# Half of the up projection by Strassen's scheme: 11 block products instead of 12, with the weight sums on VectorE

## The chip, the cores and the metric

One Trainium2 chip, one core. The metric is the device time of one execution, in microseconds (us).

## The reference, cut to what matters

One layer of a streaming encoder runs for 256 prompt frames and 8 x 16 sample frames, 384 tokens in all, in float32. The change lies in the last third, the feed-forward part:

```
h2 = rmsnorm(x, norm_ffn_g)                       # 384 x 2048
up = h2 @ w_up                                    # 2048 x 11264
g_half, u_half = up[..., :5632], up[..., 5632:]   # gate, up
gc = causal_dwconv(g_half with state, ffn_dw_w, ffn_dw_b)   # 3 taps
x  = x + (silu(gc) * u_half) @ w_down             # 5632 x 2048
```

Everything before it (norm, one combined projection, a convolution branch, attention, an output projection `w_out`) stays as it is, except for what the `w_out` stage prepares.

## The kernel before, in words

The 384 tokens are three tiles of 128. A float32 product is made from three matmuls: every operand is split into a part `hi` in the reduced matmul format and a remainder `lo`, and hi x hi, hi x lo and lo x hi are added up in PSUM (lines 235 to 237). Activations stand as the stationary operand (128 x 128, one load per matmul), weights stream past as the moving operand (512 columns).

Weights come as **items**: 256 rows by 512 columns, 512 KB, in the order of the list `plan`. `fetch` (L124) loads an item into one of three `raw` buffers, on SP's queue. `split` (L135) makes `hi` by a cast on ScalarE (L139) and `lo` by a subtraction on VectorE (L140); there are two `hi`/`lo` pairs. `ahead(2)` (L190) keeps one item split while TensorE uses another. An item is worth 2 K blocks x 3 token tiles x 3 = 18 matmuls.

The feed-forward part (from L957) goes over 11 groups of 512 gate and 512 up columns. `up_jobs` (L1031) makes the gate half of a group in 8 items, then the up half in 8 items; ScalarE takes each PSUM tile out with the norm's scale (L1039). The rows are then turned (`turned`, L261): three transposes of 32 x 32 blocks on VectorE (L249), four DMAs to DRAM (L254) and one back (L259), both issued by GpSimd. On the turned gate, `fill` (L983) copies rows on ScalarE (L987) and GpSimd (L990 to L994), and `taps` (L997) does the convolution on VectorE (L1006, L1008) and the Silu on ScalarE. `product` (L1019) multiplies gate and up and splits the result on VectorE (L1022, L1027) and ScalarE. `after(n, fn)` has a step emitted n ticks later; a tick is 9 matmuls. The down projection (`down_jobs`, L1043) runs after groups 4, 8 and 10, over four, four and three groups; VectorE adds its PSUM tiles to `y` (L1047).

In the `w_out` stage, `wo_job` (L922) turns each 512 columns of the residual, scales them, and splits them into `xg` (L939 to L942), the stationary operand of the up projection.

TensorE's order is that of the program. The other engines' order is set by a scheduler when the kernel is built: by priority (`SPLIT_AHEAD`, `EVAC_AHEAD`) and by its own idea of when things are ready. On the chip each engine then runs its list strictly in that order.

Of the kernel before, what the change touches and what calls it, by code (L numbers as in the profile page):

```python
# [33 lines left out]
SPLIT_AHEAD, EVAC_AHEAD = 150, 60  # L34

# [5 lines left out]
def hybrid_step(  # L41
# [92 lines left out]

    def split(raw, o, by_row=False):  # L135
        hi = wp.tile([P, 2, 512], F32R, tag="hi", bufs=2, name="hi")
        lo = wp.tile([P, 2, 512], F32R, tag="lo", bufs=2, name="lo")
# [6 lines left out]

    def planned(w, k0, cols, nk, *more):
        for k in range(k0, k0 + nk, 2):
            for cl in (cols,) + more:
                plan.append([w[0, k * P:(k + 2) * P, c:c + n].rearrange("(k p) n -> p k n", p=P) for c, n in cl])

    def up_cols(g):  # L150
        return [[(512 * g, 512)], [(DFF + 512 * g, 512)]]
# [21 lines left out]
    for what, g in FFN_PLAN:  # L173
        if what == "up":
            for cols in up_cols(g):
                planned(w_up, 0, cols, 16)
# [13 lines left out]
    def ahead(n):  # L190
        while plan and len(ready) < n:
            with tc.high_priority(offset=SPLIT_AHEAD):
                if x_left and (len(plan) - v_last) in range(3, 14, 2):
                    load_x(x_left.pop(0), 2)
                ready.append(split(*fetch(plan.pop(0))))
# [16 lines left out]
    def gemm(jobs, sides=()):  # L212
        for js in jobs:
# [4 lines left out]
            for j, k in [(j, k + i) for k in range(0, js[0]["nk"], 2) for j in js for i in range(2)]:  # L218
                nb, n, nk, ps = len(j["ps"]), j["n"], j["nk"], j["ps"]
                kk = k % 2  # L220
                if kk == 0:
                    ahead(2)
                    hi, lo = ready.pop(0)
# [682 lines left out]
    xg = [p_x2.tile([P, 2, 4, NT], F32R, name=f"xg{g}") for g in range(4)]  # L906
    p_w, close_w = pool("norm2", side="right")
    ss2 = p_w.tile([P, NTT, 4], F32, name="ss2")
    r2 = p_w.tile([P, NTT], F32, name="r2")
    y = []  # L910
# [10 lines left out]

    def wo_job(n):  # L922
        box = []

        def ev(t, ps):
# [4 lines left out]
            jk = p_w.tile([P, 512], F32, tag="jk", bufs=1, name="jk2")  # L930
            nc.scalar.activation(jk[:], ys, AF.Square, accum_out=ss2[:, t, n:n + 1])

        def done():
            d = box[0].moved()

            def parts(m):
                v = d[:, :, :, m, :]
                g = col[:, R_FFN + 4 * n + m:R_FFN + 4 * n + m + 1]
                hi, lo = natural(xg[n][:, 0, m, :]), natural(xg[n][:, 1, m, :])  # L939
                nc.scalar.activation(v, v, AF.Identity, scale=g)  # L940
                nc.scalar.copy(hi, v)
                tt(lo, v, f(hi), op=ALU.subtract)  # L942
            for m in range(4):
                after(3 + m // 2, lambda m=m: parts(m))
            if n == 3:
                second_norm()
        return job("B", 16, grouped(mix), ev, done=done)

    def second_norm():
# [3 lines left out]
        newton_rsqrt(r2[:], p_w.tile([P, NTT], F32, name="r2s")[:], m2[:])  # L953

# [4 lines left out]
    sft = p_f.tile([P, 44, 32], F32, name="sft")  # L959
# [6 lines left out]
    quadrants_in(sft[:].rearrange("p a c -> p (a c)"), quadrants_out(sw, 352))  # L966
# [139 lines left out]
```

## Time and profile before

| | |
|---|---|
| median of 3 runs | 1996.56 us (1995.78 to 1997.12) |
| profiled execution, its time | 1996.37 us |
| its span | 1994.7 us |
| TensorE busy | 1986.0 us of the span, 9386 matmuls |
| VectorE busy | 1063.9 us, 53% |
| ScalarE busy | 769.8 us, 39% |
| GpSimd busy | 211.1 us, 11% |
| moved by DMA | 339.31 MB, 170 GB/s on average |
| granted TensorE clock | 1.0 in every slice |

The feed-forward part begins at about 912 us and lasts to the end. A mean duration of an instruction is that of its record, from its start to its end; two that follow each other on VectorE can overlap a little in the record. The time of a run is 1.7 us above its span.

### The profile page before, as it was taken

The numbers are of one execution on the slowest core, as the hardware profiler recorded it, in microseconds if no ns is written. First come the engines' busy times: TensorE is split into PE (matmuls) and PEld (weight loads), VectorE is DVE, ScalarE is ACT, GpSimd is POOL, SyncE is SP. The second block draws the span as 40 slices with busy tenths as digits, with TensorE's granted clock in tenths as the row PEclk, the third lists the DMA queues.
The fourth block names the chain that finished last, engine by engine and source line by source line (L and its number), as shares of the span: only waits on it lengthen the run. The fifth ranks groups of instructions, "written<-read, shape, count | busy, mean of one in ns | idle before, by whom it ended". The sixth has DMA issues, their size and how long they took to land.

```text
span 1994.7 us, 24618 instructions
## 1 busy us (share of the span) xinstructions
PE 1986.0 (100%) x9386; PEld 1675.8 (84%) x9386; DVE 1063.9 (53%) x1492; ACT 769.8 (39%) x1134; POOL 211.1 (11%) x470
## 2 busy tenths in 40 slices
PE   9999999999999999999999999999999999999999
PEld 9999888888888888888888888888888888888887
DVE  4478889647456347445454555343554554334543
ACT  5433354554325323445343434222433442223422
POOL 1001121100000002011211112000211120002100
PEclk9999999999999999999999999999999999999999
DMA  6565776664444448566656565444555564346553
GB/s 183 155 170 159 230 240 209 204 179 136 126 132 122 132 149 277 179 192 173 216 160 193 164 193 168 150 132 131 175 175 177 181 185 134 128 131 194 162 186 121
DMA packets 190781, 339.31 MB, mean 170 GB/s; under 512 B 15342, under 2 KB 65513, under 8 KB 190655
## 3 DMA queue, kind: packets, MB, share of 16 engines
q1 hardware_dynamic: 173175, 273.19, 45.1%
q0 software_dynamic: 17168, 64.42, 10.3%
q8 instruction: 73, 1.20, 0.3%
q14 instruction: 45, 0.37, 0.1%
q10 hardware_dynamic: 320, 0.14, 0.0%
HBM read 298.64 MB, written 39.51 MB: 170 GB/s over the span
## 4 chain that ended last, share of the span: by engine, by line
PE 96%; DVE 3%; issue 1%; DMA 0%; SPq 0%; POOL 0%; ACT 0%; DVEq 0%; POOLq 0%
PE acc L236 28%; PE acc L235 28%; PE acc L237 28%; PE acc L232 2%; PE acc L230 2%; PE acc L231 2%; DVE ut L500 1%; DVE lo L140 1%; PE misc L235 1%; PE misc L236 1%; PE misc L237 1%; PE misc L299 0%; DMA kc<-in_cache_k_dram 0%; PE misc L711 0%; PE misc L744 0%
## 5 line engine op out<-in xcount | busy, mean ns | idle before, releaser
L140 DVE TENSOR_TENSOR lo<-raw,hi 128x1024 fp32r<-128x1024 f32 (+2 forms) x481 | 579.5, 1205 | 816.9 <-ACT hi L139 816.8
L139 ACT CAST hi<-raw 128x1024 fp32r<-128x1024 f32 (+2 forms) x481 | 498.8, 1037 | 1069.2 <-PE acc L237 897.3
L236 PE MATMUL acc<-lo,xg 128*128 128x512 f32 x1056 | 410.9, 389 | 0.1
L237 PE MATMUL acc<-hi,xg 128*128 128x512 f32 x1056 | 410.8, 389 | 0.0
L235 PE MATMUL acc<-hi,xg 128*128 128x512 f32 x1056 | 410.8, 389 | 0.0
L235 PE MATMUL acc<-hi,hT 128*128 128x512 f32 (+1 forms) x704 | 270.4, 384 | 0.1
L236 PE MATMUL acc<-lo,hT 128*128 128x512 f32 (+1 forms) x704 | 265.6, 377 | 1.1 <-DVE lo L140 0.9
L237 PE MATMUL acc<-hi,hT 128*128 128x512 f32 (+1 forms) x704 | 265.6, 377 | 0.0
L236 PEld LDWEIGHTS acc<-lo,xg 128*128 128x128 f32 x1056 | 198.3, 188 | 41.8 <-DVE lo L140 0.5
L235 PEld LDWEIGHTS acc<-hi,xg 128*128 128x128 f32 x1056 | 198.3, 188 | 41.1
L237 PEld LDWEIGHTS acc<-hi,xg 128*128 128x128 f32 x1056 | 198.3, 188 | 40.9
L236 PE MATMUL acc<-lo,act 128*128 128x512 f32 x484 | 188.3, 389 | 0.0
L235 PE MATMUL acc<-hi,act 128*128 128x512 f32 x484 | 188.3, 389 | 0.0
L237 PE MATMUL acc<-hi,act 128*128 128x512 f32 x484 | 188.3, 389 | 0.0
L254 POOL DMA_DIRECT2D turn<-block x124 | 67.9, 554 | 929.7 <-DVE block L249 903.6
L236 PEld LDWEIGHTS acc<-lo,hT 128*128 128x128 f32 x704 | 132.3, 188 | 24.0 <-DVE lo L140 2.8
L235 PEld LDWEIGHTS acc<-hi,hT 128*128 128x128 f32 x704 | 132.2, 188 | 24.0 <-issue 1.8
L500 DVE SCALAR_TENSOR_TENSOR ut<-ext,cw,ut 128x384 f32<-128x384 f32 x240 | 149.1, 621 | 5.5
L237 PEld LDWEIGHTS acc<-hi,hT 128*128 128x128 f32 x704 | 132.1, 188 | 22.9
L235 PEld LDWEIGHTS acc<-hi,act 128*128 128x128 f32 x484 | 90.9, 188 | 18.9
L237 PEld LDWEIGHTS acc<-hi,act 128*128 128x128 f32 x484 | 90.9, 188 | 18.8
L236 PEld LDWEIGHTS acc<-lo,act 128*128 128x128 f32 x484 | 90.9, 188 | 18.8
(296 smaller groups left out, 2126.5 us busy)
## 6 DMA issues: line engine op xcount, KB each, us to landing
raw<-in_w_up_dram SPq DMA_DIRECT2D x176, 512.0 KB
raw<-in_w_in_dram SPq DMA_DIRECT2D x96, 512.0 KB
raw<-in_w_down_dram SPq DMA_DIRECT2D x88, 512.0 KB
turn<-block POOLq DMA_DIRECT2D x120, 192.0 KB, 4.2
block<-turn POOLq DMA_DIRECT2D x30, 768.0 KB, 5.7
raw<-in_w_in_dram SPq DMA_DIRECT2D x64, 256.0 KB
raw<-in_w_out_dram SPq DMA_DIRECT2D x32, 512.0 KB
raw<-in_w_att_out_dram SPq DMA_DIRECT2D x16, 512.0 KB
```

The costliest lines, as they stand in the source:

```text
L139: nc.scalar.copy(hi[:, k, :o], raw[:, k, :o])
L140: tt(lo[:, k, :o], raw[:, k, :o], f(hi[:, k, :o]), op=ALU.subtract)
L230: mm(o, hi[:, kk, s], ah, start=st, stop=False)
L231: mm(o, hi[:, kk, s], al, start=False, stop=False)
L232: mm(o, lo[:, kk, s], ah, start=False, stop=sp)
L235: mm(o, ah[:, s], hi[:, kk, :n], start=st, stop=False)
L236: mm(o, ah[:, s], lo[:, kk, :n], start=False, stop=False)
L237: mm(o, al[:, s], hi[:, kk, :n], start=False, stop=sp)
L254: nc.gpsimd.dma_start(d[:, :, i, :].rearrange("j r n -> r j n"), src[32 * i:32 * i + 32, :].rearrange("r (j n) -> r j n", j=4))
L500: stt(o, v, wc, o, op0=ALU.mult, op1=ALU.add)
```

## The change

In 2 of the 4 blocks of 512 K rows (`MIXED`, blocks 0 and 1) the gate and up columns of a group are computed together. Token tiles 0 and 1, the two K pairs of the block and the column halves gate/up form a 2 x 2 by 2 x 2 block product, which takes 7 block products instead of 8; token tile 2 keeps its 4. So 12 become 11, and per mixed block and group 72 matmuls become 66.

- **Activations.** `combined` makes the five sums of token blocks once, in the `w_out` stage, and splits them and the five plain blocks into `xm`. Only blocks 2 and 3 keep `xg`.
- **Weights.** `planned_mixed` makes 7 items of a mixed block where there were 4. Four of the seven are sums, added on VectorE before the split (`both`, `top`, `grown` twice). A mixed block takes 5 loads instead of 4 (one is loaded twice). Items now carry 12, 12, 6 (first phase), 12, 6 (second), 12, 6 (third) matmuls; items of blocks 2 and 3 still 18.
- **Buffers.** There is a third `hi`/`lo` pair, and `ahead(3)` in the feed-forward part.
- **Order.** A group runs in three phases: up columns with the sums (10 items, 132 matmuls), products that both halves need (4 items, 36), gate columns (8 items, 108). A group is 22 items and 276 matmuls, where it was 16 and 288. The K blocks go 0, 2, 1, 3.
- **Evacuation.** Results are put together from PSUM by nine VectorE steps and seven ScalarE steps per group, where there were six on ScalarE.
- **Down.** The down projection now runs over two groups at a time (four times) and three at the end: 60 PSUM tiles to add instead of 36. So groups 1, 2, 4, 6, 8 and 10 begin right behind another group, the other four behind a down projection.

```diff
+        def both(q):
+            sums[q] = new_sum[0](q)
+            tt(sums[q], held["b22"][:], single("b12", 4 * q, c2)[:], op=ALU.add)
+            return sums[q]
+
+        def top(q):
+            b = single("b11", 4 * q, c1)
+            tt(b[:], b[:], held["b12"][:], op=ALU.add)
+            return b
+
+        def grown(q, name):
+            tt(sums[q], sums[q], held[name][:], op=ALU.add)
+            return sums[q]
+
+        for q in ORDER:
+            if q in MIXED:
+                add(lambda q=q: single("b22", 4 * q + 2, c2))
+                add(lambda q=q: both(q))
+                add(lambda q=q: top(q))
+            else:
+                planned(w, 4 * q, [(c2, 512)], 4)
+        for q in MIXED:
+            add(lambda q=q: single("b11", 4 * q, c1))
+            add(lambda q=q: grown(q, "b11"))
+        for q in ORDER:
+            if q in MIXED:
+                add(lambda q=q: single("b21", 4 * q + 2, c1))
+                add(lambda q=q: grown(q, "b21"))
+            else:
+                planned(w, 4 * q, [(c1, 512)], 4)
...
-    FFN_PLAN = [("up", g) for g in range(5)] + [("down", (0, 1, 2, 3))]
-    FFN_PLAN += [("up", g) for g in range(5, 9)] + [("down", (4, 5, 6, 7))]
-    FFN_PLAN += [("up", g) for g in range(9, 11)] + [("down", (8, 9, 10))]
+    FFN_PLAN = [("up", 0)]
+    for n in range(0, 8, 2):
+        FFN_PLAN += [("up", n + 1), ("up", n + 2), ("down", (n, n + 1))]
+    FFN_PLAN += [("up", 9), ("up", 10), ("down", (8, 9, 10))]
...
+        def add_up():
+            box.append(block()[:, :1280].rearrange("p (j m n) -> p j m n", j=5, m=2))
+            s = [blocks(box[0][:, j]) for j in range(5)]
+            tt(s[0], of(1, 1), of(1, 0), op=ALU.subtract)
+            tt(s[1], of(0, 0), s[0], op=ALU.add)
+            tt(s[2], of(0, 1), s[1], op=ALU.subtract)
+            tt(s[3], of(0, 0), of(1, 0), op=ALU.subtract)
+            tt(s[4], of(2, 1), of(2, 0), op=ALU.subtract)
...
+        def q3(ps):
+            stt(rows("u")[:, 0], ps, scale[0], e0, op0=ALU.mult, op1=ALU.subtract)
+
+        def q2(ps):
+            stt(rows("u")[:, 1], ps, scale[1], e1, op0=ALU.mult, op1=ALU.subtract)
...
+        def q6(ps):
+            with tc.high_priority(offset=EVAC_AHEAD):
+                tt(e0, ps, e1, op=ALU.subtract)
+            for r, sc in ((rows("u")[:, 0], scale[0]), (rows("u")[:, 1], scale[1]),
+                          (rows("g")[:, 1], nr2[:, 1:2])):
+                stt(r, e0, sc, r, op0=ALU.mult, op1=ALU.add)
+            ups[g] = Turned(block, rows("u")).moved().rearrange("p i t q c -> p (i t) q c")
...
+        for q in ORDER:
+            if q in MIXED:
+                seq += [pairs(q, ("q3", 2), ("tu", 4)), pairs(q, ("p7", 3), ("tu", 8)), pairs(q, ("p5", 0))]
+            else:
+                seq += plain(q, "q3", "q2", "tu")
...
+            if q in MIXED:
+                seq += [pairs(q, ("tg", 9), ("p2", 6)), pairs(q, ("q4", 7))]
+            else:
+                seq += plain(q, "p2", "q4", "tg")
```

Two places show how VectorE's list moves. The first is a gate's convolution, in the middle of the stretch in which the next group runs. In the rows of before, `lo<-raw,hi` is the subtraction of a split and `gc` a tap; four splits stand ahead of the first tap:

```order
L140 TENSOR_TENSOR lo<-raw,hi 128x1024 x4
L1006 TENSOR_SCALAR gc<-extf_7701,fw,col 128x384
L1006 TENSOR_SCALAR gc<-extf_7702,fw,col 128x384
L1008 SCALAR_TENSOR_TENSOR gc<-extf_7701,fw,gc 128x384
L1006 TENSOR_SCALAR gc<-extf_7703,fw,col 128x384
L1006 TENSOR_SCALAR gc<-extf_7704,fw,col 128x384
L1008 SCALAR_TENSOR_TENSOR gc<-extf_7702,fw,gc 128x384
L140 TENSOR_TENSOR lo<-raw,hi 128x1024
```

And of the change, where L149 is the same subtraction, L186 a sum `grown`, L1106 and L1108 the taps:

```order
L1106 TENSOR_SCALAR gc<-extf_7716,fw,col 128x384
L1106 TENSOR_SCALAR gc<-extf_7717,fw,col 128x384
L186 TENSOR_TENSOR sums<-sums,raw 128x1024
L149 TENSOR_TENSOR lo<-raw,hi 128x1024
L1106 TENSOR_SCALAR gc<-extf_7718,fw,col 128x384
L149 TENSOR_TENSOR lo_6749<-raw,hi_6748 128x1024
L186 TENSOR_TENSOR sums<-sums,raw 128x1024
L1106 TENSOR_SCALAR gc<-extf_7719,fw,col 128x384
L1108 SCALAR_TENSOR_TENSOR gc<-extf_7716,fw,gc 128x384
L1108 SCALAR_TENSOR_TENSOR gc<-extf_7717,fw,gc 128x384
L149 TENSOR_TENSOR lo<-sums,hi 128x1024
```

What moved: splits and sums now stand between the taps, and from the first tap to the split of the group's 21st item there are 44 instructions in a row (16 splits and sums, 12 taps, 8 product steps, 8 evacuation steps).

The second place is the start of the feed-forward part, where the last block of the residual, `xg_6751`, is split (L942 before, L1032 in the change). Before:

```order
L115 TENSOR_TENSOR r_6756<-r_6756,r2s 128x3
L140 TENSOR_TENSOR lo<-raw,hi 128x1024 x5
L942 TENSOR_TENSOR xg_6751<-block,xg_6751 128x4x3x32 x4
L140 TENSOR_TENSOR lo<-raw,hi 128x1024 x2
L249 STREAM_TRANSPOSE block<-block 128x11x4x32
```

The change:

```order
L1046 TENSOR_SCALAR nr_6761<-r_6760 128x3
L149 TENSOR_TENSOR lo<-raw,hi 128x1024 x2
L186 TENSOR_TENSOR sums<-sums,raw 128x1024
L149 TENSOR_TENSOR lo_6749<-raw,hi_6748 128x1024
L149 TENSOR_TENSOR lo<-raw,hi 128x1024
L186 TENSOR_TENSOR sums<-sums,raw 128x1024
L1032 TENSOR_TENSOR xg_6751<-block,xg_6751 128x4x3x32 x4
L149 TENSOR_TENSOR lo<-sums,hi 128x1024
```

What moved: the split of `xg_6751` now stands behind the splits of items 7 to 10 of the first group (counted from 0), while item 8 is the first that uses `xg_6751`.

## Rows read from the trace of the kernel before

**Rows 1.** The page: busy times of TensorE and VectorE, and the chain that ended last.
```profile
PE 1986.0 (100%) x9386; PEld 1675.8 (84%) x9386; DVE 1063.9 (53%) x1492; ACT 769.8 (39%) x1134; POOL 211.1 (11%) x470
...
PE 96%; DVE 3%; issue 1%; DMA 0%; SPq 0%; POOL 0%; ACT 0%; DVEq 0%; POOLq 0%
```

**Rows 2.** Windows: stretch, then busy us (count) by engine, clock, DMA share, GB/s.
```profile
1100.00:1200.00 100.00, 100.00 (x443) 82.84 (x442) 51.75 (x67) 41.01 (x54) 14.49 (x33) 1.00 0.59 178
...
1300.00:1400.00 100.00, 100.00 (x443) 82.83 (x442) 37.24 (x37) 26.38 (x25) 0.00 (x0) 1.00 0.42 131
```

**Rows 3.** All waits of TensorE: line, releaser, us in total, times, longest.
```profile
PE misc L318 <- POOL ident masks.py:199: 2.5, 1, 2.5
PE acc L236 <- DVE lo L140: 0.9, 3, 0.5
PE acc L232 <- DVE lo L140: 0.5, 1, 0.5
```

**Rows 4.** Groups by form, 1000 to 1994 us: busy us, mean ns, idle before.
```profile
L140 DVE TENSOR_TENSOR lo<-raw,hi 128x1024 fp32r<-128x1024 f32 x242 | 296.3, 1224 | 493.7 <-ACT hi L139 493.7
L139 ACT CAST hi<-raw 128x1024 fp32r<-128x1024 f32 x242 | 255.2, 1055 | 577.8 <-PE acc L237 497.9 <-PE misc L237 57.5 <-issue 22.0
...
L1008 DVE SCALAR_TENSOR_TENSOR gc<-extf,fw,gc 128x384 f32<-128x384 f32 x80 | 45.7, 612 | 0.0
...
L249 DVE STREAM_TRANSPOSE block<-block 128x512 f32<-128x512 f32 x60 | 41.9, 709 | 22.1 <-ACT block L1039 22.1
...
L1027 DVE TENSOR_TENSOR act<-ac,act 128x384 fp32r<-128x384 f32 x44 | 22.6, 553 | 1.2
L1047 DVE TENSOR_TENSOR y<-acc,y 128x512 f32<-128x512 f32 x33 | 22.6, 691 | 9.0 <-PE acc L237 9.0
...
L1006 DVE TENSOR_SCALAR gc<-extf,fw,col 128x384 f32<-128x384 f32 x40 | 19.1, 478 | 6.4 <-POOL extf L994 5.7
```

**Rows 5.** VectorE's timeline, 1144 to 1169 us: start, us, instruction, idle before.
```profile
1144.06 0.70 DVE L249 STREAM_TRANSPOSE block<-block 128x512 f32<-128x512 f32 x1
...
1159.24 1.22 DVE L140 TENSOR_TENSOR lo<-raw,hi 128x1024 fp32r<-128x1024 f32 x1 [2.85 <-ACT hi L139]
1160.82 1.04 DVE L1006 TENSOR_SCALAR gc<-extf,fw,col 128x384 f32<-128x384 f32 x2 [0.35 <-POOL extf L994]
...
1163.91 1.22 DVE L140 TENSOR_TENSOR lo<-raw,hi 128x1024 fp32r<-128x1024 f32 x1
1165.05 2.73 DVE L1008 SCALAR_TENSOR_TENSOR gc<-extf,fw,gc 128x384 f32<-128x384 f32 x5
1167.69 1.22 DVE L140 TENSOR_TENSOR lo<-raw,hi 128x1024 fp32r<-128x1024 f32 x1
```

**Rows 6.** The turn's DMAs to DRAM (after L254) and back (after L259): time to landing.
```profile
DMA to landing us min/median/max: 3.1/4.2/6.0
...
DMA to landing us min/median/max: 4.4/5.6/6.9
```

**Rows 7.** GpSimd's timeline at the same gate's fill, then all 44 instructions of L992.
```profile
1159.73 0.79 POOL L992 COPY extf<-extf 128x16 f32<-128x16 f32 x1 [6.83 <-ACT extf L987]
1160.46 0.19 POOL L993 COPY extf<-extf 128x12 f32<-128x12 f32 x1
...
L992 POOL COPY extf<-extf x44: 193/394/842, 971.6 to 1879.9; 128x16 f32<-128x16 f32 x44
```

**Rows 8.** VectorE at the start of the feed-forward part, then the first use of xg.
```profile
935.59 2.13 DVE L942 TENSOR_TENSOR xg<-block,xg 128x384 fp32r<-128x384 f32 x4
...
L235 PE MATMUL acc<-hi,xg x55: 389/389/390, 912.8 to 949.5; 128*128 128x512 f32 x55
```

**Rows 9.** SP's queue, 1100 to 1900 us; then the page: GB/s in 40 slices.
```profile
SPq L130 <- DVE lo L140: 680.2, 189, 4.2
...
GB/s 183 155 170 159 230 240 209 204 179 136 126 132 122 132 149 277 179 192 173 216 160 193 164 193 168 150 132 131 175 175 177 181 185 134 128 131 194 162 186 121
```

More of the change, by code (lines that the diff above doesn't have):

```diff
@@ L147, in planned, with planned_mixed, add, single @@
             for cl in (cols,) + more:
-                plan.append([w[0, k * P:(k + 2) * P, c:c + n].rearrange("(k p) n -> p k n", p=P) for c, n in cl])
-    def up_cols(g):
-        return [[(512 * g, 512)], [(DFF + 512 * g, 512)]]
+                plan.append([rows_of(w, k, c, n) for c, n in cl])
+    sums, new_sum = {}, []
+    ORDER = [q for n in range(4) for q in (MIXED[n:n + 1] + tuple(sorted(set(range(4)) - set(MIXED)))[n:n + 1])]
+    def planned_mixed(w, c1, c2):
+        held = {}
+        def add(fn):
+            plan.append(lambda: split(fn(), 512))
+        def single(name, k, c):
+            held[name] = fetch([rows_of(w, k, c, 512)])[0]
+            return held[name]
+        def both(q):
[25 more added lines that the diff above has]
+                planned(w, 4 * q, [(c1, 512)], 4)
     V_COLS = [[(O_V + 344 * i, 344)] for i in range(3)]
@@ L194, in ahead @@
                     load_x(x_left.pop(0), 2)
-                ready.append(split(*fetch(plan.pop(0))))
+                item = plan.pop(0)
+                ready.append(item() if callable(item) else split(*fetch(item)))
     def grouped(tiles):
@@ L997, in taps @@
             def taps():
-                gcs = gates[g] = [p_f.tile([P, NT], F32, tag="gc", bufs=6, name="gc") for _ in range(4)]
+                gcs = gates[g] = [p_f.tile([P, NT], F32, tag="gc", bufs=4, name="gc") for _ in range(4)]
                 for w in range(3):
@@ L1011, in done @@
             after(5, taps)
+            after(7, lambda: product(g))
         return done
[L1014 to L1029 removed]
@@ L1031, in up_jobs, with product @@
-    def up_jobs(g):
-        def half(finish):
-            box = []
-            def ev(t, ps):
-                if t == 0:
-                    rows = block()[:].rearrange("p (t n) -> p t n", t=NTT)
-                    box.append(Turned(block, rows))
-                nc.scalar.activation(box[0].rows[:, t, :], ps[:], AF.Identity, scale=r2[:, t:t + 1])
-            return job("B", 16, xa, ev, done=finish(g, box))
-        return [half(up_g_done), half(up_u_done)]
+    def product(g):
+        act = acts[g] = gp.tile([P, 2, 4, NT], F32R, tag=f"G{1 + g % 3}", name=f"act{g}")
+        for m in range(4):
+            a = gates[g][m][:]
+            ac = a.rearrange("p (a c) -> p a c", c=32)
+            tt(ac, ups[g][:, :, m, :], ac, op=ALU.mult)
+            av = a.rearrange("p (i t c) -> p i t c", i=4, t=NTT)
+            hi, lo = natural(act[:, 0, m, :]), natural(act[:, 1, m, :])
+            nc.scalar.copy(hi, av)
+            tt(lo, av, f(hi), op=ALU.subtract)
@@ new lines, in hybrid_step, with run @@
+    spent = [0]
+    def run(seq, forms, bank, finish, open_=()):
+        last = {b: (i, n) for i, prods in enumerate(seq) for n, (b, _, _) in enumerate(prods)}
+        for i, prods in enumerate(seq):
+            ahead(depth[0])
+            hi, lo = ready.pop(0)
+            for n, (b, (ah, al), kk) in enumerate(prods):
+                st = b not in forms
+                if st:
+                    forms[b] = bank()
+                o = forms[b][:]
+                mm(o, ah, hi[:, kk, :], start=st, stop=False)
+                mm(o, ah, lo[:, kk, :], start=False, stop=False)
+                mm(o, al, hi[:, kk, :], start=False, stop=last[b] == (i, n) and b not in open_)
+            for b in last:
+                if last[b][0] == i:
+                    finish[b](forms[b][:])
+            spent[0] += len(prods)
+            while spent[0] >= 3:
+                spent[0] -= 3
+                tick(())
```

142 lines of the change are left out of this document (108 added, 34 removed).

## The prediction

> **What bounds the kernel now.** I read the page first: TensorE is busy over the whole span, and the chain that ended last is TensorE for 96% [rows 1]. The windows then show how fast it goes in the feed-forward part: 443 matmuls in 100 us at full clock, whether VectorE is busy for 52 or for 37 of them [rows 2]. That is 225.7 ns per matmul. The list of its waits shows that it practically never stands: 1.4 us in total for splits of VectorE [rows 3]. So matmuls are the price, and a matmul less is 225.7 ns less as long as the weights are split in time. VectorE's groups show the slack: before its 242 splits it idled 493.7 us, waiting for casts, and the casts idled 577.8 us, almost all of it until TensorE gave a buffer free [rows 4]. SP's loads, too, wait for splits, not the other way round [rows 9].
>
> **The change part by part.**
>
> *Matmuls.* 6 fewer per mixed block, 2 blocks, 11 groups: 132. 132 x 225.7 ns = **29.8 us less**.
>
> *Splits and sums.* 3 more splits and 4 sums per mixed block: 66 more casts, 66 more subtractions, 88 sums. A split costs VectorE 1.224 us and ScalarE 1.055 us [rows 4]; the sum has the same 1024 elements, and I give it 1.224 us as well. That is 14 x 1.224 = 17.1 us more of VectorE per group. Beside it come nine evacuation steps per group that VectorE did not have: an addition from PSUM takes 0.69 us [rows 4], and the multiply-and-add forms I put at 0.75, since on 384 elements that form takes 612 ns where a product step takes 553; 6.5 us. ScalarE gets 6 casts and one evacuation more per group, some 7 us, and its casts idled for more than half of the time. Nothing of this is on TensorE's path by itself. What hides it is the time that an item gives: a buffer comes free when TensorE ends the item three before, then 1.055 us of cast and 1.224 us of subtraction follow. An item used to be 18 x 0.2257 = 4.06 us; now there are items of 12 (2.71 us) and 6 (1.35 us).
>
> *Where that cover gets thin.* In six groups (1, 2, 4, 6, 8, 10) the gate of the group before is turned, filled and convolved inside the next group's items, which the order shows. I add up VectorE's list there, from the first tap to the split of item 20: 16 splits and sums 19.6 us, 8 taps of 612 ns 4.9 us, 4 of 478 ns 1.9 us, 8 product steps 4.4 us [rows 4], one transpose 0.7, two additions 1.4, five multiply-and-adds 3.75: **36.7 us**. TensorE's cover in the same stretch: VectorE is done with split 8 at the earliest 2.4 us after item 5 ends (cast, split, a hop of 0.1), and item 20 is due after items 6 to 19, which are 162 matmuls, 36.6 us: 34.2 us of cover. By full durations 2.5 us are missing. But records overlap: five taps in a row end with the next instruction starting 2.64 us after the first, 528 ns each where the record says 612, and a split that began at 1163.91 is followed at 1165.05, 1.14 us later [rows 5]. That is 85 ns less for each of 44: 3.7 us, so 33.0 us, and **1.2 us of slack**. I take this value, since it is measured on the same forms back to back, and keep 2.5 us missing as the other end.
>
> The Trainium skill speaks against it: "VectorE: DVE Perf Modes", section "The DRAIN you can't avoid", says that the next instruction does not start until the pipe of the one before is empty. By that rule the full durations count and the stall is 2.5 us per group; the trace has the next start inside the record of the last.
>
> *The gate's taps come late, too.* Between the last transpose of a gate and its first tap lie the turn through DRAM and the fill. Before: the transpose ends at 1144.76, the first tap starts at 1160.82, 16.1 us [rows 5]. In the change the transposes end about 4.4 us after the group (two evacuations of 0.75, three transposes of 0.71, a split of 1.22 between them, less 85 ns each), so taps can begin 20.5 us after it; VectorE reaches them after items 0 to 5 (78 matmuls, 17.6 us) plus 2.4, at 20.0. That is 0.5 us of standing. Landing varies: 3.1 to 6.0 us out, 4.4 to 6.9 back, medians 4.2 and 5.6 [rows 6]; with 18 loads in a 62 us group instead of 16 in 65 I take half the way to the maxima, 1.55 us more. So 2.05 us late against 1.2 us of slack: 0.85 us of stall, six times, **5 us more** (bounds: 0, and 2.5 + 0.5 + 3.1 = 6.1 each, 37 us).
>
> *Start of the feed-forward part.* The last four steps of the residual's split now stand behind split 10 on VectorE, and split 10 needs the buffer of item 7; item 8 needs that residual. So after item 7 TensorE waits for a cast, a split and one step: 1.055 + 1.224 + 0.55 + hops, **3.0 us more**, once. Before, that split ran at 935.6 to 937.7 us, 23 us after the first up matmul at 912.8, when it was due after 12 K blocks (108 matmuls, 24.4 us) [rows 8]; now it is due after 96 (21.7 us). Bounds 0 to 4.
>
> *The w_out stage.* Two residual blocks get 11 steps on VectorE instead of 4. Nine of 256 elements and one of 1280 stand between two splits: by the 1.14 us of 1024 and the 470 ns of 384, some 4.4 to 5.3 us. The splits there come every 4.06 us with 1.8 us to spare. 0 to 0.6 us each, I take **0.6 us more** in all.
>
> *Costed at nothing.* The 24 more additions of the down projection (0.69 us each) fall into stretches where VectorE is busy for 37 of 100 us [rows 2]; if the cover were gone they would cost 17 us. The 22 more loads of 512 KB wait in SP's queue for buffers: three raw buffers are now held for the sums, so the loads come in bunches, three in 30 matmuls (6.8 us), 232 GB/s, and one slice of before has 277 GB/s with TensorE busy throughout [rows 9]. SP's small stores of gate rows stand where the raw buffer of the next load is still held, so they hold up nothing. The last down projection needs the last group's product after 8 items (32.5 us), and by the chain above it is ready at about 31.8: 0 to 3 us, taken as 0.
>
> Sum: -29.8 + 5 + 3.0 + 0.6 = -21.2. Against the profiled execution, 1996.37 us (0.2 below the median of the runs): **1975 us**.
>
> **The rivals.**
>
> *A. VectorE's instructions do not overlap in this list* (chance 0.17). This is the rule cited above. Waits between engines stand between most of them, and the overlap of rows 5 is one of instructions that waited for nothing. Then 2.5 + 0.5 = 3.0 us per group, with half the landings 4.5: 18 to 27 us. -29.8 + 3.6 + 22 = -4: 1992 us. For it: full records. Against it: the 1.14 us of a split among taps.
>
> *B. The gate comes late, and VectorE's list blocks on it* (chance 0.12): slower. The first tap stands in front of splits in a list that runs strictly in order, so each microsecond that a gate is late beyond the slack is a microsecond of TensorE, six times. It decides from (29.8 + 4.0 - 3.6) / 6 = 5 us of stall per group. Landings at their maxima give 3.1 us. GpSimd's fill gives the rest: a copy of 0.19 us took 0.79 us when a split ran on VectorE, and ended as the split ended; the 44 copies of that line lie between 193 and 842 ns [rows 5, 7]. Four copies stand ahead of the first tap, each up to 1.14 us later: 4.6 us. 0.5 + 3.1 + 4.6 - 1.2 = 7.0 per group, 42 us: -29.8 + 3.6 + 42 = +16, 2012 us. Against it: VectorE stands idle between splits 7 and 8, just when the fill runs.
>
> The Trainium skill, "SBUF — State Buffer", section "SBUF: two separate sides", has a rule for such copies: a GpSimd instruction and a VectorE instruction with two inputs in SBUF exclude each other for a whole instruction. The trace agrees, with 0.79 us beside a split.
>
> *C. The loads come late* (chance 0.06). Of 22 bunches of three loads each costs 1 us: -21.2 + 22, 1997 us. Against it: SP waits only for splits, 680 us in 800 [rows 9].
>
> *D. All is hidden* (chance 0.10): 1996.4 - 29.8 = 1966.6 us.
>
> **How the numbers follow.** The forecast has 0.55, with a range of its own of 1967 to 1985. A measurement of this kernel can tell 0.2% from no change, 4.0 us. Faster by more: forecast, D and about 0.10 of A, 0.75. Within: the rest of A and most of C, 0.12. Slower: B and a little of C, 0.13. The range, 1966 to 1994, holds the forecast, A and D, 0.82.
>
> **What would show it.** The page should count about 9254 matmuls (9386 before); a window inside a down projection still has 443 matmuls in 100 us. TensorE's waits should name the split's subtraction (L149) for some 5 us in groups 1, 2, 4, 6, 8, 10 at their items 12 to 20, and the residual's split (L1032) once for about 3 us. VectorE's busy time should be near 1063.9 + 154 x 1.22 + 24 x 0.69 + 99 x 0.72 = 1340 us, two thirds of the span. Waits on VectorE for GpSimd before the first tap should be about 0.5 to 2 us in those groups; 7 us there would be rival B. Subtractions that follow taps at 1.22 us and not 1.14 would be rival A. The prediction is wrong if TensorE waits over 15 us in all, or if a matmul takes longer than 226 ns among the short items.

## The result, and the profile after

The changed kernel takes 2007.18 us (median of 5 runs, 2003.84 to 2007.23), the kernel before 1996.56 us (5 runs beside it). The ratio is 1.0048, with a 95% interval from 1.0033 to 1.0062: slower by half a per cent, about 10 us. The forecast was 1975 us, and with it faster. The profiled execution took 2007.18 us, its span 2005.5 us against 1994.7 us before: 10.8 us more.

The page: busy times of the engines, and the chain that ended last, as in [rows 1].

```profile
PE 1973.6 (98%) x9254; PEld 1652.7 (82%) x9254; DVE 1317.8 (66%) x1784; ACT 841.5 (42%) x1216; POOL 227.6 (11%) x470
...
PE 80%; DVE 11%; DMA 5%; issue 2%; POOL 1%; ACT 1%; SPq 0%; DVEq 0%; POOLq 0%; ACTq 0%
```

The 132 matmuls are gone (9254 of 9386), but 20% of the chain is no longer TensorE; before it was 4%. What TensorE waited for (line, releaser, us in total, times, longest), against [rows 3]:

```profile
PE acc L289 <- DVE y L1233: 9.9, 8, 1.8
PE acc L1139 <- DVE lo L149: 5.3, 7, 2.2
PE acc L1138 <- ACT xg L1031: 3.0, 1, 3.0
PE misc L1139 <- DVE lo L149: 2.9, 5, 0.8
...
PE acc L1140 <- DVE xg L1032: 1.3, 1, 1.3
```

The largest wait is one that the forecast had put at nothing: the first matmuls of a job of the down projection (L289) wait for the additions of y (L1233), which let a PSUM bank go. The splits (L149, 8.2 us in the two rows shown) come second, the late residual (L1031, L1032) third. The windows of the changed kernel, as in [rows 2]: the first five stages of the feed-forward part, and two stretches inside them.

```profile
914.20:1111.80 197.60, 192.25 (x830) 156.44 (x829) 158.09 (x190) 100.45 (x129) 37.26 (x71) 0.98 0.63 197
1111.80:1183.10 71.30, 68.95 (x289) 55.72 (x288) 40.52 (x53) 22.67 (x29) 9.12 (x22) 0.95 0.50 167
1183.10:1309.40 126.30, 125.53 (x554) 103.55 (x553) 95.94 (x107) 58.97 (x69) 13.88 (x30) 1.00 0.57 175
1309.40:1378.00 68.60, 66.04 (x289) 53.79 (x288) 40.41 (x53) 22.68 (x29) 9.11 (x22) 1.00 0.52 169
1378.00:1507.20 129.20, 126.98 (x553) 103.24 (x552) 95.64 (x107) 58.91 (x69) 16.57 (x30) 1.00 0.55 171
...
939.70:946.50 6.80, 5.34 (x12) 3.79 (x13) 4.11 (x6) 3.47 (x8) 0.00 (x0) 0.50 0.52 161
...
1147.90:1154.70 6.80, 6.25 (x15) 4.46 (x14) 4.37 (x8) 0.65 (x2) 0.00 (x0) 0.50 0.24 77
```

A down projection of two groups has 288 matmuls and takes 65.3 us where nothing waits (e4, below), 226.7 ns for each; here the first takes 71.3 us and the other three 68.7. And the granted clock, 1.00 throughout the kernel before, is 0.50 in two stretches of 6.8 us and one of 3.4 us (from 1864.7): 1.2 GHz instead of 2.4. Each goes with a stand of TensorE: one of 3.2 us that ended at 939.8, one of 1.9 that ended at 1146.3, one of 2.3 that ended at 1864.3. In the stretches of 6.8 us the windows count 12 and 15 matmuls, where full clock gives 30; in the first of them TensorE also stood for another 1.7 us.

All runs can be read by one table, worked out from the profiled executions: the time from the first matmul of a stage to the first of the next, the four two-group downs added up, and groups 3 to 10 as well. The first line is e4 (below), which has the stages of the change with the matmuls of before, less 226.7 ns for each that the change removes: what the change would take if nothing waited more. Each line is one execution. The runs of one kernel lie 1 to 9 us apart, so differences of 2 or 3 us outside the downs can be chance.

| kernel | stage starts | groups 0 to 2 | four downs | groups 3 to 10 | last down |
|---|---|---|---|---|---|
| e4 less removed matmuls | 912.6 | 188.1 | 261.1 | 500.5 | 97.9 |
| the change | 914.2 | 197.6 | 277.4 | 513.4 | 98.4 |
| e1 | 912.2 | 197.7 | 261.1 | 508.3 | 98.4 |
| e12 | 913.2 | 200.2 | 261.1 | 510.3 | 98.3 |
| e2 | 912.9 | 196.2 | 277.4 | 510.4 | 98.4 |
| e3 | 912.4 | 207.6 | 266.2 | 515.2 | 97.9 |
| e5 | 912.5 | 196.3 | 261.1 | 509.8 | 98.3 |
| e6 | 912.9 | 197.6 | 261.1 | 507.9 | 97.9 |
| e7 | 912.3 | 195.6 | 261.1 | 510.5 | 98.4 |
| e8 | 913.2 | 195.4 | 261.1 | 508.9 | 98.4 |
| e9 | 913.9 | 195.8 | 261.1 | 505.6 | 97.9 |
| e10 | 912.1 | 195.5 | 261.1 | 506.8 | 98.4 |
| e11 | 912.0 | 194.8 | 261.1 | 504.2 | 97.9 |

So the change saves 29.9 us of matmuls and gives back 16.3 us in the downs, 12.9 in groups 3 to 10, 9.5 in groups 0 to 2 and 2.1 at the two ends: +10.9 us, where the spans say 10.8.

### The profile page after: what moved, and what is told of

The parts are those of the page before. It is cut to its first block, busy times and chain, and to the rows that moved or that the text cites. A ratio compares the mean times of both kernels' runs of the same rounds, so it can differ in the third digit from the quotient of the medians.

```text
span 2005.5 us, 24794 instructions
## 1 busy us (share of the span) xinstructions
PE 1973.6 (98%) x9254; PEld 1652.7 (82%) x9254; DVE 1317.8 (66%) x1784; ACT 841.5 (42%) x1216; POOL 227.6 (11%) x470
## 4 chain that ended last, share of the span: by engine, by line
PE 80%; DVE 11%; DMA 5%; issue 2%; POOL 1%; ACT 1%; SPq 0%; DVEq 0%; POOLq 0%; ACTq 0%
PE acc L289 15%; PE acc L291 15%; PE acc L290 15%; PE acc L1140 6%; PE acc L1139 6%; PE acc L1138 6%; DVE lo L149 4%; DMA raw<-in_w_up_dram 3%; PE misc L1139 3%; PE misc L1140 3%; PE misc L1138 2%; DVE ut L554 2%; PE acc L286 2%; PE acc L284 1%; PE acc L285 1%
## 5 line engine op out<-in xcount | busy, mean ns | idle before, releaser
L149 DVE TENSOR_TENSOR lo<-raw,hi 128x1024 fp32r<-128x1024 f32 (+2 forms) x481 | 577.2, 1204 | 505.7 <-ACT hi L148 503.3
L289 PE MATMUL acc<-hi,hT 128*128 128x512 f32 (+1 forms) x704 | 270.4, 384 | 0.1
L290 PE MATMUL acc<-lo,hT 128*128 128x512 f32 (+1 forms) x704 | 266.2, 378 | 1.3 <-DVE lo L149 1.2
L289 PE MATMUL acc<-hi,act 128*128 128x512 f32 x484 | 190.8, 394 | 10.0 <-DVE y L1233 9.9
L1139 PE MATMUL acc<-lo,xg 128*128 128x512 f32 x440 | 173.4, 394 | 3.8 <-DVE lo L149 3.7
L1138 PE MATMUL acc<-hi,xg 128*128 128x512 f32 x440 | 173.4, 394 | 3.1 <-ACT xg L1031 3.0
L1140 PE MATMUL acc<-hi,xg 128*128 128x512 f32 x440 | 172.8, 393 | 1.3 <-DVE xg L1032 1.3
L289 PEld LDWEIGHTS acc<-hi,hT 128*128 128x128 f32 x704 | 132.2, 188 | 24.0 <-issue 1.8
L148 ACT CAST hi<-sums 128x1024 fp32r<-128x1024 f32 x66 | 69.4, 1051 | 127.3 <-PE misc L1140 43.5
L1139 PE MATMUL acc<-lo,xm 128*128 128x512 f32 x308 | 120.3, 391 | 1.6 <-DVE lo L149 1.6
L1138 PE MATMUL acc<-hi,xm 128*128 128x512 f32 x308 | 119.9, 389 | 0.0
L1140 PE MATMUL acc<-hi,xm 128*128 128x512 f32 x308 | 119.9, 389 | 0.0
L289 PEld LDWEIGHTS acc<-hi,act 128*128 128x128 f32 x484 | 91.5, 189 | 33.9 <-ACT hi L148 8.6
```

The lines of the kernel that those rows point to most:

```text
L148: nc.scalar.copy(hi[:, k, :o], raw[:, k, :o])
L149: tt(lo[:, k, :o], raw[:, k, :o], f(hi[:, k, :o]), op=ALU.subtract)
L289: mm(o, ah[:, s], hi[:, kk, :n], start=st, stop=False)
L290: mm(o, ah[:, s], lo[:, kk, :n], start=False, stop=False)
L1138: mm(o, ah, hi[:, kk, :], start=st, stop=False)
L1139: mm(o, ah, lo[:, kk, :], start=False, stop=False)
```

## The experiments

Line numbers shift with the edits; the operation and the names say which line is meant.

### The down projection: e4, e1, e12

e4 is the kernel before with the change's `FFN_PLAN` (its diff stands above).

> The kernel before with nothing changed but the grouping of the down projections (pairs of groups instead of four, four and three). It has 24 more additions and pairs of jobs that end after 8 items instead of 16, but its taps lie in the second half of a group and its products early in the down, some 20 us ahead of the pair's end. Theory (it is the meeting of taps and products with the end of the pair that costs): 1996 to 1999 us, waits for additions under 2 us in all. Rival (smaller downs cost by themselves, by additions or bank release): 2006 to 2010 us, four pairs of gaps as in the changed kernel.

Measured: 1996.10 us, ratio 1.0001 (0.9992 to 1.0010). The list of waits has none of TensorE in the feed-forward part, and the down takes 65.3 us:

```profile
1108.80:1174.10 65.30, 65.30 (x290) 54.09 (x289) 32.25 (x38) 19.47 (x22) 2.74 (x5) 1.00 0.48 154
```

So neither the 24 additions nor the smaller downs cost anything that can be measured by themselves. One thing of the expectation was off: the products come at 1127 to 1133 us, and the pair's first additions at 1136.2, some 3.5 us later and not 20.

In the changed kernel they meet. VectorE there, in the first two-group down (start, us, instruction): 

```profile
1139.84 2.73 DVE L1108 SCALAR_TENSOR_TENSOR gc<-extf,fw,gc 128x384 f32<-128x384 f32 x5
1142.49 1.02 DVE L1120 TENSOR_TENSOR gc<-block,gc 128x384 f32<-128x384 f32 x2
1143.43 1.22 DVE L149 TENSOR_TENSOR lo<-raw,hi 128x1024 fp32r<-128x1024 f32 x1
1144.56 1.02 DVE L1124 TENSOR_TENSOR act<-gc,act 128x384 fp32r<-128x384 f32 x2
1145.50 0.68 DVE L1233 TENSOR_TENSOR y<-acc,y 128x512 f32<-128x512 f32 x1
1146.10 0.55 DVE L1120 TENSOR_TENSOR gc<-block,gc 128x384 f32<-128x384 f32 x1
1146.57 0.68 DVE L1233 TENSOR_TENSOR y<-acc,y 128x512 f32<-128x512 f32 x1
1147.17 1.21 DVE L149 TENSOR_TENSOR lo<-raw,hi 128x1024 fp32r<-128x1024 f32 x1
1148.30 0.68 DVE L1233 TENSOR_TENSOR y<-acc,y 128x512 f32<-128x512 f32 x1
```

And TensorE:

```profile
1144.19 0.39 PE L291 MATMUL misc<-hi,act 128*128 128x512 f32 x1
1146.33 0.47 PE L289 MATMUL acc<-hi,act 128*128 128x512 f32 x1 [1.75 <-DVE y L1233]
...
1149.04 0.80 PE L289 MATMUL acc<-hi,act 128*128 128x512 f32 x1 [0.55 <-DVE y L1233]
```

The first bank of the pair's first job was complete at 1139.1 (the end of its last matmul), but its addition stands behind taps, splits and product steps until 1145.50, and the second and third are pulled apart by another product step and a split. The pair holds all five banks of its pool and one of the other, so the third job's three banks are those of the first: it starts 1.91 us late, when the first addition is done, and waits 0.93 us more for the third. The same pair of gaps comes back in the other three downs, at 1343.9, 1541.8 and 1739.2.

e1 takes the need for that bank away:

```diff
-        return [(jobs[0], jobs[1])] + jobs[2:]
+        return [(jobs[0], jobs[1])] + jobs[2:] if last else jobs
...
-                j["ps"] = [(misc_tile if j is not js[0] and i == 2 else acc_tile)() for i in range(nb)]
+                j["ps"] = [(misc_tile if (j is not js[0] or j["spread"]) and i == 2 else acc_tile)()
```

> The changed kernel, but the four two-group down projections run their four column jobs one after the other (not the first two interleaved), and each job takes its third bank from the other PSUM pool, so that a job's first matmul never needs a bank that the job just before it still holds. Theory (bank release behind taps and products on VectorE): the four pairs of gaps of 1.91 and 0.93 us before L289 go, 11.4 us, and with them the half-clock stretch after 1146 (3.4 us): 2007 to 1992-1996 us, no wait of TensorE for the additions of y over 0.3 us. Rival 1 (VectorE has simply too much to do there, so the lateness moves on to the splits): the waits for the additions go, waits for splits in the same downs take their place, time within 3 us of 2007. Rival 2 (the clock falls whatever TensorE waits for): gaps go, three half-clock stretches stay, about 1996.

Measured: 1986.86 us (1984.01 to 1987.67), ratio 0.9957 (0.9940 to 0.9973): 20 us less than the change, more than expected. The gaps and the half-clock stretch in the first down are gone, 16.3 us in the table, and no other wait has come in their place there, so rival 1 falls. Of the three half-clock stretches one stays, at 938 us, so rival 2 falls as well. Groups 3 to 10 are 5 us shorter too, among other things without the half-clock stretch at 1864.7; why they vary by a few us between kernels that are alike there was not traced.

e12 leaves the banks and moves the taps:

```diff
-            after(5, taps)
-            after(7, lambda: product(g))
+            wait = 16 if g in (2, 4, 6, 8) else 0
+            after(5 + wait, taps)
+            after(7 + wait, lambda: product(g))
...
+                            if g in (2, 4, 6, 8):
+                                tc.add_manual_dep(d.ins, pair_end[0], mybir.DependencyInfo(
+                                    mybir.DependencyClass.NoSync, mybir.DependencyReason.DATA), reason="queue")
```

> The changed kernel with nothing but this: in the groups that a down projection follows (2, 4, 6, 8), taps and products stand behind the additions of the down's first pair of jobs on VectorE. Banks, pairing and the number of additions stay as in the changed kernel. Theory (the meeting of taps and products with the end of the pair is what costs): the four pairs of gaps of 1.91 and 0.93 us before L289 fall under 0.3 us, as in e4_plan_alone, and the half-clock stretch after 1146 goes: 1992 to 1997 us. Rival (the pair's five plus one banks are too few in the changed kernel, whenever the taps come): gaps stay, 2005 to 2008 us.

Measured: 1988.63 us, ratio 0.9956 (0.9940 to 0.9973), some 3 us below the range that was expected: the downs alone give back 16.3 us, where 14.8 had been added up from gaps and clock, and the rest was not traced. The downs take 65.3 us each, with the same six banks and the same additions. VectorE's list there, with the additions (L1238) now in front:

```profile
1140.81 2.05 DVE L1238 TENSOR_TENSOR y<-acc,y 128x512 f32<-128x512 f32 x3 [0.41 <-PE acc L291]
...
1144.89 1.37 DVE L1238 TENSOR_TENSOR y<-acc,y 128x512 f32<-128x512 f32 x2 [0.41 <-PE acc L291]
1146.25 0.69 DVE L1238 TENSOR_TENSOR y<-misc,y 128x512 f32<-128x512 f32 x1
1146.86 0.86 DVE L1107 TENSOR_SCALAR gc<-extf,fw,col 128x384 f32<-128x384 f32 x2
```

The additions start as their matmuls end. So it is the order in VectorE's list at the end of the pair that costs, and either cure, other banks or later taps, is enough.

### The start: e2, e5

ScalarE in the changed kernel, where the last block of the residual has been on its way back since 929.8:

```profile
936.01 1.05 ACT L148 CAST hi<-raw 128x1024 fp32r<-128x1024 f32 x1 [2.13 <-DMA raw<-in_w_up_dram]
937.30 1.04 ACT L148 CAST hi<-raw 128x1024 fp32r<-128x1024 f32 x1 [0.24 <-DMA raw<-in_w_up_dram]
938.25 1.12 ACT L1028 ACTIVATE block<-block,col 128x384 f32<-128x384 f32 x2
939.27 0.91 ACT L1031 CAST xg<-block 128x384 fp32r<-128x384 f32 x2
```

The residual's steps (L1028, L1031) stand behind two casts that themselves waited for loads. e2 orders the splits from the tenth item on, and the sums beside them, behind those steps on both engines:

```diff
+    def behind(d):
+        if last_part and len(skipped) >= 3:
+            tc.add_manual_dep(d.ins, last_part[d.ins.engine], mybir.DependencyInfo(
+                mybir.DependencyClass.NoSync, mybir.DependencyReason.DATA), reason="queue")
...
-            nc.scalar.copy(hi[:, k, :o], raw[:, k, :o])
-            tt(lo[:, k, :o], raw[:, k, :o], f(hi[:, k, :o]), op=ALU.subtract)
+            behind(nc.scalar.copy(hi[:, k, :o], raw[:, k, :o]))
+            behind(tt(lo[:, k, :o], raw[:, k, :o], f(hi[:, k, :o]), op=ALU.subtract))
```

> The changed kernel, with the splits of the items from the tenth on (and the sums beside them) ordered behind the last residual split on ScalarE and VectorE, at the start of the feed-forward part only. Theory (the residual's split stood behind casts and a sum that waited for late loads): the two gaps of 3.16 and 1.74 us at 940 us shrink to one of 1.5 to 2.5 us, since the turned residual lands at about 936; the half-clock stretch of 6.8 us there goes as well: 2007 to 1999-2002 us. Rival (the residual itself is late, its place in the list costs nothing): 2005-2007 us, gaps and half-clock stretch stay.

Measured: 2000.51 us, ratio 1.0027 (1.0016 to 1.0037). ScalarE reaches the residual at 936.09, and what TensorE waited for there is this:

```profile
PE acc L1151 <- ACT xg L1043: 2.2, 1, 2.2
PE acc L1151 <- ACT block L1192: 1.7, 1, 1.7
```

The gaps of 3.16 and 1.74 us became one of 2.35, and the half-clock stretch at 940 us, worth some 2.4 us, did not come. But two new gaps did: 1.16 us at 943.4, behind a split, and 1.88 us at 960, where an evacuation on ScalarE (L1192) now stands behind the casts that were held back. So groups 0 to 2 are shorter by 1.4 us only. The medians differ by 6.7 us; the rest of what the two profiled executions show lies ahead of group 0 (1.3) and in groups 3 to 10 (3.0), and is not shown to come from the edit.

e5 is e1 and e2 together.

> The edits of e1_down_single and e2_start_order together. If the two costs are separate they add: 20 us (e1) and 6.7 us (e2) below 2007: 1980 us, no half-clock stretch inside the feed-forward part or one at most, and about 12 us of TensorE's gaps left, most of them in groups 2, 4, 6, 8 and 10. Rival (the stalls of the start were only covered up by something that now comes to light): 1984 us or more.

Measured: 1983.33 us, ratio 0.9938 (0.9923 to 0.9953), no stretch of half clock before TensorE's last matmul. That is 3.5 us less than e1 where 6.7 were expected, near the rival's bound, and the intervals of e1 and e5 overlap: how much the second edit adds is open.

### The groups behind another group: e3, e6 to e11

VectorE stands waiting for loads in the changed kernel (its waits after 910 us), where before it had no such row:

```profile
DVE raw L182 <- DMA raw<-in_w_up_dram: 29.5, 16, 5.0
DVE sums L177 <- DMA raw<-in_w_up_dram: 14.1, 10, 3.6
```

and L186 adds 11.6 us. In groups 6, 8 and 10 most of TensorE's lost time comes behind such a stand. In group 10, VectorE and then TensorE:

```profile
1861.85 1.23 DVE L186 TENSOR_TENSOR sums<-sums,raw 128x1024 f32<-128x1024 f32 x1 [2.21 <-DMA raw<-in_w_up_dram]
1862.99 1.22 DVE L149 TENSOR_TENSOR lo<-raw,hi 128x1024 fp32r<-128x1024 f32 x1
1864.26 0.50 PE L1139 MATMUL acc<-lo,xg 128*128 128x512 f32 x1 [2.17 <-DVE lo L149]
```

The split of item 9 had its cast done at 1860.24, but stands behind a sum that waits for its load; TensorE stands for 2.3 us, and the half-clock stretch of 3.4 us follows. In groups 4, 6 and 8 TensorE waits at item 12 as well, 0.93 us each time, and there VectorE's list has run without a break since its first taps (groups 6 and 8) or the sum behind them (group 4). So two causes were open: late loads (theory L), or a list on VectorE that is too long (theory V). e3 adds a fourth buffer:

```diff
-        raw = wp.tile([P, 2, 512], F32, tag="raw", bufs=3, name="raw")
+        if fourth:
+            fourth.append(0)
+        if fourth and len(fourth) % 4 == 0:
+            raw = fourth[0]
+        else:
+            raw = wp.tile([P, 2, 512], F32, tag="raw", bufs=3, name="raw")
...
+    fourth.append(p_f.tile([P, 2, 512], F32, name="raw4")[:])
```

> The changed kernel with a fourth buffer for loaded weights in the feed-forward part, in room that three constants of earlier stages leave. Theory (a load of a mixed block is issued only when a sum has let a buffer go, and the sum of the next buffer then waits for it, so load latency lies in series): VectorE's waits for loaded weights (55 us on L177, L182 and L186) fall under 15 us, the stalls of groups 2, 4, 6, 8 and 10 fall from about 10 us to 3 or less: 2007 to 1998-2002 us; the gaps in the downs stay. Rival (VectorE's own time is short there, as by full durations): waits for loads fall, the stalls stay, 2005-2007 us.

Measured: 2007.68 us, ratio 1.0061 (1.0046 to 1.0076): nothing gained in all. The waits for loads did not fall; they rose to 91 us, and the order of the list moved too: the downs are 11.2 us shorter than in the change, groups 0 to 2 10.0 longer. VectorE in e3, group 10:

```profile
1845.72 1.22 DVE L155 TENSOR_TENSOR lo<-sums,hi 128x1024 fp32r<-128x1024 f32 x1
1853.84 1.23 DVE L192 TENSOR_TENSOR sums<-sums,raw 128x1024 f32<-128x1024 f32 x1 [6.90 <-DMA raw<-in_w_up_dram]
1854.98 2.35 DVE L155 TENSOR_TENSOR lo<-raw,hi 128x1024 fp32r<-128x1024 f32 x2
```

A sum that isn't due yet waits 6.9 us for its load, and two splits that are due stand behind it. So e3 tells nothing between L and V. e7 keeps splits and sums in the order of their items, e8 adds the fourth buffer to it:

```diff
+        e = d.ins.engine
+        if third and e in in_list:
+            tc.add_manual_dep(d.ins, in_list[e], mybir.DependencyInfo(
+                mybir.DependencyClass.NoSync, mybir.DependencyReason.DATA), reason="queue")
+        if third:
+            in_list[e] = d.ins.name
```

> e5 with the splits and weight sums of the feed-forward part kept in the order of the items on VectorE and ScalarE (no sum ahead of a split of an earlier item). Theory L1 (a sum that waits for a late load stands ahead of splits that are due first, as at 1853.8 in e3_raw4): VectorE's waits of sums for loads fall from 50 to under 35 us, 2 to 5 us less than e5. Theory V: within 2 us of e5.

> e7 with the fourth buffer for loaded weights of e3_raw4. Theory L2 (load latency lies in series behind the sums, and e3 lost what it won only by its order): VectorE's waits for loads under 20 us, 4 to 8 us less than e7. Theory V: waits for loads fall, the time is within 2 us of e7.

Measured: e7 1985.36 us, ratio 0.9949 (0.9934 to 0.9964); e8 1983.12 us, 0.9936 (0.9919 to 0.9952). Neither differs from e5, so the gains that L1 and L2 had forecast did not come. In e7 VectorE's waits for loads fell to 14 us, and in e8 the list of its waits has no row with a load at all. TensorE's waits at items 2 to 9 of groups 1 to 10 are gone in both. But now it waits at items further on, in e8 twice in each of groups 4, 6, 8 and 10. Group 6 of e8, which begins at 1429.2, VectorE and then TensorE:

```profile
1448.16 1.22 DVE L171 TENSOR_TENSOR lo<-raw,hi 128x1024 fp32r<-128x1024 f32 x1 [1.50 <-ACT hi L170]
1450.05 1.04 DVE L1136 TENSOR_SCALAR gc<-extf,fw,col 128x384 f32<-128x384 f32 x2 [0.66 <-POOL extf L1124]
...
1453.23 0.48 DVE L1136 TENSOR_SCALAR gc<-extf,fw,col 128x384 f32<-128x384 f32 x1 [0.48 <-POOL extf L1124]
...
1455.90 0.47 DVE L1136 TENSOR_SCALAR gc<-extf,fw,col 128x384 f32<-128x384 f32 x1
1456.29 1.67 DVE L1138 SCALAR_TENSOR_TENSOR gc<-extf,fw,gc 128x384 f32<-128x384 f32 x3
1457.88 1.22 DVE L171 TENSOR_TENSOR lo<-sums,hi 128x1024 fp32r<-128x1024 f32 x1
1459.01 2.20 DVE L1138 SCALAR_TENSOR_TENSOR gc<-extf,fw,gc 128x384 f32<-128x384 f32 x4
1461.13 1.02 DVE L1150 TENSOR_TENSOR gc<-block,gc 128x384 f32<-128x384 f32 x2
...
1465.94 1.21 DVE L171 TENSOR_TENSOR lo<-sums,hi 128x1024 fp32r<-128x1024 f32 x1
...
1467.21 0.50 PE L1169 MATMUL misc<-lo,xm 128*128 128x512 f32 x1 [0.85 <-DVE lo L171]
1471.90 0.50 PE L1169 MATMUL acc<-lo,xm 128*128 128x512 f32 x1 [0.31 <-DVE lo L171]
```

From the last idle time, ahead of the tap at 1453.23, VectorE works without a break, and the split that TensorE waits for is the last of it. That is theory V, in the items numbered 13 and 15 (they begin with the 163rd and 181st matmul of the group). The list's start counts beside its length: VectorE stood 0.66 and 0.48 us for GpSimd's copies ahead of taps, and no run moves those copies. e6 takes the four first taps off VectorE, e9 does the same with the loads in time, e10 puts the products later, e11 does both:

```diff
-                            ts(o, v, wc, col[:, R_FDB + c:R_FDB + c + 1], op0=ALU.mult, op1=ALU.add)
+                            nc.scalar.activation(o, v, AF.Identity, scale=wc,
+                                                 bias=col[:, R_FDB + c:R_FDB + c + 1])
...
-            after(7, lambda: product(g))
+            after(7 if g == 10 else 14, lambda: product(g))
```

> e5 with the first of the three taps (four instructions of 0.47 us per group on VectorE) computed on ScalarE instead. Theory V (in groups behind another group VectorE's list between the gate's arrival and the short items of the middle phase is longer than TensorE's cover): 1.9 us less list, so the two gaps of about 0.9 us in each of those groups shrink or go: 4 to 8 us less than e5. Theory L (late loads set those gaps): within 2 us of e5.

> e8, whose VectorE no longer waits for loads, with the first tap on ScalarE as in e6: 1.9 us less of VectorE's list per group. Theory V (with the loads in time, VectorE's list from the gate's arrival to the end of the short items is what TensorE waits for): the two gaps of 0.8 to 1.0 us in each of groups 4, 6, 8 and 10 shrink by 1 to 1.8 us per group: 1975 to 1979 us. Rival (the gaps come from the cast and split of a short item itself, whatever else stands in the list): within 2 us of e8.

> e8 with the product of gate and up (8 steps, 4.3 us on VectorE per group) emitted 7 units of 9 matmuls later (not in the last group), so that most of it stands behind the splits of the short middle items. Theory V: the same work, but out of the tight stretch, so the gaps of groups 4, 6, 8 and 10 shrink as with less work: 1975 to 1980 us. Rival (the sum of VectorE's work counts, not its place): within 2 us of e8.

> e9 and e10 together. Theory V: the gaps of groups 2 to 10 all but go; what stays over the bound of 29.8 us less than before (1966) is the start of the feed-forward part (4 to 5 us) and about 2 us elsewhere: 1972 to 1976 us. Rival (something else than VectorE's list, the evacuations or ScalarE, sets the rest): 1979 us or more.

Measured: e6 1985.20 us, ratio 0.9948 (0.9933 to 0.9963), no gain over e5; e9 1978.71 us, 0.9912 (0.9896 to 0.9929), as expected; e10 1980.82 us, 0.9924 (0.9909 to 0.9938), and e11 1976.70 us, 0.9903 (0.9888 to 0.9918), each just above the range expected. The same 1.9 us off the list, with the same start and the same downs, give nothing that can be measured where loads are late (e6) and 4.4 us where they are in time (e9 against e8, whose intervals just overlap). With the first taps on ScalarE, the tied order and the fourth buffer are worth 6.5 us, and e6 and e9 lie apart with their whole intervals; without that they are worth nothing that can be measured (e8 against e5). So both theories hold, one behind the other: at e5 taking away either cause alone shows the other. What of it is the order and what the fourth buffer was not taken apart: no run has the tap on ScalarE with the order alone. That the place of the work counts as well as its amount is not shown: e10 has e8's work and is 2.3 us below it, but their intervals overlap.

e11 is the fastest version, 19 us below the kernel before. What TensorE still waits for in its feed-forward part:

```profile
PE acc L1170 <- DVE lo L171: 3.5, 7, 0.8
...
PE acc L1169 <- ACT block L1210: 1.8, 1, 1.8
PE misc L1170 <- DVE lo L171: 0.6, 1, 0.6
```

## Why the prediction was wrong, point by point

- **What bounds the kernel, and the matmuls: right.** 9254 matmuls, and the same time for each as before, among the short items as well. That time is 226.7 ns from start to start, not 225.7: the 443 matmuls of a window count those that lie across its edges, as the window of 65.3 us of e4 counts 290 of its 288. So the sign "longer than 226 ns" was already there before and tells nothing. The saving, 29.9 us, is there: once most of the costs below are taken away, in e11, the time is 1976.7 us.
- **The down projection, costed at nothing: the step that failed most, 16.3 us.** The prediction weighed VectorE's busy share, 37 in 100 us, over a whole down. But the change put two things in the same 12 us of it: a pair of jobs now ends after 8 items and no longer after 16, and the taps and products of the group before come late. It named no bank that waits for an addition. e4, e1 and e12 show that this meeting is all of it. "If the cover were gone they would cost 17 us" was nearly the result, but by chance and by another mechanism: not additions laid end to end but one bank held 6 us too long, four times, and a clock that fell.
- **The clock: not in the prediction.** Waits were priced at their own length. But 17.1 us at half clock followed or went with three of them, and each matmul done in that time took 0.43 us from start to start instead of 0.23. In the first down this is 2.7 us (71.3 against 68.7 us in the other three, with the same waits), over all about 6.7.
- **Six groups, 5 us forecast: the mechanism is there, the size agrees by luck.** Groups 1, 2, 4, 6, 8 and 10 of the changed kernel lose 14.7 us, against matmuls at 226.7 ns. About 5 of them lie at items 12 to 20, where the forecast put them and for the reason it gave. The other 9.7 lie at items 2 to 9 of groups 6, 8 and 10 (next point). Those earlier waits hold TensorE back, so the list has more time behind them. Without them, in e8, it costs 1.9 to 2.0 us in each of groups 4, 6, 8 and 10, where 0.85 was forecast. The slack was drawn up over the whole stretch from the first tap to item 20; in e8 it runs out earlier, at items 13 and 15, in or after the short middle items: 36 matmuls, 8.2 us, with four splits, two sums and the evacuations between.
- **Loads, costed at nothing, and rival C: a term that failed as well.** VectorE stood 55 us for them, where SP had been seen to wait for splits alone. Most of the 9.7 us follow such stands, 1.6 of it as clock (group 10, above). Rival C had the cause, at 1 us for each of 22 bunches, but not the place. Taken away alone they gained nothing, since the list then sets the time (e8 against e5).
- **Start, 3.0 us forecast: right place, 8.0 us in group 0.** The residual was late by 3.16 + 1.74 us, not 3.0; about 2.4 us are the clock and 0.7 a split at 920.4. The longer wait was for ScalarE's part of the residual (L1031), which stood behind casts that waited for loads; the forecast had put 3 us on VectorE's (L1032). The table's 9.5 us hold 1.9 of groups 1 and 2 too, and e4 itself waits 0.4 there.
- **Rival A.** A tap that began at 1455.90 with a record of 0.47 us is followed at 1456.29 (e8), 0.39 us later, and the split behind the taps at 1457.88 is followed at 1459.01, 1.13 us later: by the sign named beforehand, not rival A. Records overlap in the long list too, and the rule of the Trainium skill cited in the prediction ("VectorE: DVE Perf Modes", "The DRAIN you can't avoid"), taken for every instruction, does not hold in this trace; the measurement decides. The same section of the Trainium skill adds "A next op that is not held starts earlier", which the prediction left out and which these rows agree with.
- **Rival B** gave the sign, and its 2012 us lie near the result by chance: VectorE waited for GpSimd ahead of taps for 5.9 us in 11 groups, 2.5 at most, not 7 in each of six. The sign that TensorE waits over 15 us in all did tell: its list adds up to 26.5 us, 2.5 of them those of before.
- **Prices.** Sums took 1.22 us and multiply-and-adds 0.745, as put. VectorE is busy for 1317.8 us, not 1340.
- **Stage of w_out:** the feed-forward part begins between 912.0 and 914.2 us in the twelve kernels that have the change's w_out stage, and at 912.8 before, so 0.6 us can't be told.

## What to carry to other kernels

When an edit halves a stage, look for what now ends at the same moment as something else, and which bank or buffer is let go there: a busy share of 37% over the stage says nothing about those few microseconds. Do the same for the loads: ask which buffer each one needs, and what in the list waits for it. Draw up the slack of an engine's list at each item that is due, not over the whole stretch, with the shortest items in view. And when a fix shows nothing, try it again with the next limit removed before it is given up: here the loads in time (a tied order and a fourth buffer) and the tap on ScalarE were each worth nothing measurable alone, and 4.6 us together.

## What the runs showed of the hardware

TensorE's granted clock fell to 0.50 during or up to 1.7 us after gaps of 1.9 to 5.3 us, for 3.4, 6.8 or 10.2 us, and never in the feed-forward part of a kernel without such a gap (e4). At half clock a matmul of 512 columns took 0.43 us from start to start, at full clock 0.23. Not each gap did it: in the changed kernel the pair of 1.91 and 0.93 us was followed by half clock at 1147.9, and by full clock in the three other downs; in e2 and e5 a gap of 2.35 us was followed by full clock, in e1 one of 2.89 us by half. What decides between them these runs do not show. Runs of one kernel differ in it, too: of the eight runs of e2 the fastest, 1996.62 us, has a mean granted clock of 0.999 and the slowest, 2005.86 us, one of 0.995.

On GpSimd, a copy of 128 x 16 elements from the state of the convolution took 507 ns in the mean before (44 of them, L990) and 898 ns in the changed kernel (L1090). Another copy of that size took 452 ns before (L992) and 394 in the change (L1092), so VectorE's denser list as the reason is not shown.
